# Two feed-forward products by one level of Strassen's algorithm

## The chip, the core and the metric

The kernel runs on one core of a Trainium2 chip. The metric is the device time of one execution in microseconds (us); of several runs the median is given. The core has five engines with queues of their own: TensorE (PE: matmuls, and weight loads that overlap them), VectorE (DVE), ScalarE (ACT), GpSimd (POOL) and SyncE (SP, which here issues DMAs). Matmuls write to PSUM, which has eight banks of 512 fp32 columns on 128 partitions; DVE and ACT read it, POOL does not here.

## The reference

The input x has 512 tokens of width 1024, in fp32. A first block (two attention branches, gated and merged) is followed by two layers, each of a feed-forward part, a mixer and a second feed-forward part, each of them with a residual and a layer norm. The change touches the four feed-forward parts:

```
def swiglu_half(x, w1, w3, w2):
    return 0.5 * ((jax.nn.silu(x @ w1) * (x @ w3)) @ w2)
...
x = layer_norm(ALPHA * x + swiglu_half(x, ffn2_w1[l], ffn2_w3[l], ffn2_w2[l]), ln3_g[l], ln3_b[l])
```

w1 and w3 are 1024 x 2816, w2 is 2816 x 1024. Everything is fp32.

## The kernel before, in words

**Products.** A full fp32 product is made of three faster ones. `split` (L212) cuts an operand into a high part, rounded to the type fp32r by ACT (L214), and the rest, a subtraction on DVE (L215). `mm3` (L248) then adds low x high, high x low and high x high in PSUM, through `mm` (L166), which all matmuls of the kernel share: in the profile they are L167 and are told apart by their tiles. The input of a layer stands transposed in `xTh` and `xTl` (features on partitions, 8 x 512 columns), made by `next_tile` (L767) with PE transposes (L307) from the residual `xr`.

**Weights.** A `Piece` (L217) loads a slab of a weight in two halves by SP's queue into `wst` and splits each half into `wh` and `wl`. In the feed-forward part w1 and w3 come from one pool (three `wst`, five `wh` and `wl` buffers, L775), w2 from another (`WP`, L238).

**Feed-forward.** The 2816 hidden features are cut into 11 blocks of 256. For a block, `hidden` computes (w1 block)^T x and (w3 block)^T x, 128 features by 512 tokens in a PSUM bank of pool `mm` at a time, 24 matmuls of 512 columns each. `act` (L787) takes Silu of the first on ACT (L788), multiplies by the second on DVE (L789) and splits the result into `hh` and `hl`. Block 0 is done apart, by halves of 256 tokens (`hidden_half`, L792), so that its first half can start before all tokens are there; after a mixer that first half lies in the mixer's tail. Then the blocks go in pairs (1,2), (3,4) to (9,10): after both, `hh` times w2 gives for each of four tiles of 128 tokens and two halves of 512 columns one bank of pool `mx`, which DVE adds to `xr` (L848). After the last pair `lnorm` (L735) does residual and norm of a tile, and `next_tile` transposes it for the next part. `banks(esf, mm=3, mx=5)` shares out the eight banks.

**Order.** The code is written in plain program order. A framework plans each engine's queue from it: an instruction goes in when its operands and its buffer (one of `bufs` under its tag) are ready by the planner's account, with earlier code first among those that are ready. It also sets the semaphores. Matmuls of a later product may thus stand between those of an earlier one. On the chip each queue is worked off in the planned order, and an instruction that has to wait holds up all that stands behind it.

Of the kernel before, what the change touches and what calls it, by code (L numbers as in the profile page):

```python
# [10 lines left out]
F32 = mybir.dt.float32  # L11
F32R = mybir.dt.float32r
# [121 lines left out]
def build(ctx, tc, A, out, stage="all"):  # L134
# [20 lines left out]
    def weights(es, nst, nw, side="left"):  # L155

        return pool(es, nm("w"), side, LINE), nst, nw

    def nm(s):
        uid[0] += 1  # L160
        return f"{s}{uid[0]}"

    def pool(es, name, side="left", line=SPAN):
        return Aligned(es.enter_context(tc.tile_pool(name=name, bufs=1, side=side, reuse_waits="tile")), line)

    def mm(o, a, b, start=True, stop=True):  # L166
        PE.matmul(o, a, b, start=start, stop=stop)  # L167

    B = {}

    def banks(es, **n):

        B.clear()
        for name, bufs in n.items():
            B[name] = es.enter_context(tc.tile_pool(name=nm("ps" + name), bufs=bufs, space=PSUM, reuse_waits="tile"))
# [4 lines left out]
    def mmbank():  # L180
        return bank("mm")

    def mxbank():
        return bank("mx")
# [27 lines left out]
    def split(hi, lo, src, eng=None):  # L212

        S.activation(hi, src, AF.Copy)  # L214
        V.tensor_sub(lo, src, hi.bitcast(F32))  # L215

    class Piece:  # L217


        def __init__(self, src, k0, nk, c0, ncol, w=None):  # L220
            wp, nst, nw = w or WP
            wp = wp.pool
            self.hk = nk // 2
            self.parts = []
            for h in range(2):
                r = (k0 + h * self.hk) * 128
                st = wp.tile([128, self.hk, ncol], F32, tag="wst", name=nm("wst"), bufs=nst)
                nc.sync.dma_start(st, src[r:r + self.hk * 128, c0:c0 + ncol].rearrange("(k p) c -> p k c", p=128))
                hi = wp.tile([128, self.hk, ncol], F32R, tag="wh", name=nm("wh"), bufs=nw)
                lo = wp.tile([128, self.hk, ncol], F32R, tag="wl", name=nm("wl"), bufs=nw)  # L230
                split(hi, lo, st)
                self.parts.append((hi, lo))
# [12 lines left out]
        for f in todo:  # L245
            f()

    def mm3(o, ah, al, bh, bl, start, stop):  # L248
        mm(o, al, bh, start, False)
        mm(o, ah, bl, False, False)  # L250
        mm(o, ah, bh, False, stop)

    def ws_block(src, c0, nm_, sink, nk=8, xh=None, xl=None):

# [38 lines left out]
    def nat(t):  # L293
        return slice(t * 128, (t + 1) * 128)
# [437 lines left out]
        return nxt  # L732


    def lnorm(t, po, scale, g, b, pl, done):  # L735

        xs = A["xr"][:, t, :]
        st = pl.tile([128, 4], F32, tag="lnst", name=nm("lnst"), bufs=2)
        s0, s1, nmu, rs = (st[:, i:i + 1] for i in range(4))
        hs = [slice(h * 512, (h + 1) * 512) for h in range(2)]  # L740
        for h in range(2):
            V.tensor_tensor_reduce(out=xs[:, hs[h]], in0=po(h), in1=xs[:, hs[h]], scale=scale, scalar=0.0 if h == 0 else s0,  # L742
                                   op0=ALU.add, op1=ALU.add, accum_out=s0 if h == 0 else s1)
        V.tensor_scalar(out=nmu, in0=s1, scalar1=-1.0 / D, scalar2=None, op0=ALU.mult)  # L744
        xn = pl.tile([128, D], F32, tag="lnx", name=nm("lnx"), bufs=1)
        sq = pl.tile([128, D], BF16, tag="lnq", name=nm("lnq"), bufs=1)
        S.activation(sq, xs, AF.Square, bias=nmu, accum_out=rs)  # L747
        powhalf(rs, rs, 1.0 / D, 1e-5)
        V.scalar_tensor_tensor(out=xn, in0=xs, scalar=nmu, in1=g, op0=ALU.add, op1=ALU.mult)
        for h in range(2):  # L750
            V.scalar_tensor_tensor(out=xs[:, hs[h]], in0=xn[:, hs[h]], scalar=rs, in1=b[:, hs[h]], op0=ALU.mult, op1=ALU.add)  # L751
            if done:
                done(t, h)
# [2 lines left out]
        hc = slice(h * 512, (h + 1) * 512)  # L756
        nc.sync.dma_start(out[0, nat(t), hc], A["xr"][:, t, hc])

    def ln_rows(pl, names, l):
        o = []  # L760
        for n in names:
            r = pl.tile([128, D], F32, name=nm("lnr"))
            nc.scalar.dma_start(r, rows(A[n][l]))
            o.append(r)
        return o
# [6 lines left out]
    def open_ffn(l, f, pre=None):  # L772

        es, w = pre[0:2] if pre else (ExitStack(), None)
        w = w or weights(es, 3, 5, "right")  # L775
        return es, w, [Piece(A[f"{f}_{n}_2"][l], 0, 8, 0, 256, wp) for n, wp in (("w1", w), ("w3", WP if pre else w))], []

    def hidden_tiles(pl, bufs):
        return tuple(pl.tile([128, 2, T], F32R, tag=n, name=nm(n), bufs=bufs) for n in ("hh", "hl"))

    def prod(o, pc, j, n0, n1):
        for k in range(8):
            wh, wl = pc.at(k)
            mm3(o, wh[:, j * 128:(j + 1) * 128], wl[:, j * 128:(j + 1) * 128], xTh[:, k, n0:n1],
                xTl[:, k, n0:n1], k == 0, k == 7)

    def act(sa, pa, pb, oh, ol):  # L787
        S.activation(sa, pa, AF.Silu)  # L788
        V.tensor_mul(sa, sa, pb)  # L789
        split(oh, ol, sa)  # L790

    def hidden_half(pl, pre, n0, bufs, sa=None):  # L792

        if not pre[3]:
            pre[3].extend(hidden_tiles(pl, bufs))
        hh, hl = pre[3]
        ab = [mmbank().rearrange("p (j n) -> p j n", j=2) for _ in range(2)]
        for i in range(2):
            for j in range(2):
                prod(ab[i][:, j, :], pre[2][i], j, n0, n0 + 256)  # L800
        sa = (pl.tile([128, T], F32, tag="sa", name=nm("sa"), bufs=2) if sa is None else sa).rearrange("p (j n) -> p j n", j=2)
        act(sa, ab[0], ab[1], hh[:, :, n0:n0 + 256], hl[:, :, n0:n0 + 256])

    def ffn(l, f, ln, pre, ahead=None, scale=None):

        w1, w3, w2 = (A[f"{f}_{w}_2"][l] for w in ("w1", "w3", "w2"))
        xr = A["xr"]
        es, wf = pre[0:2]
        nxt = None
        esf = ExitStack()  # L810
        banks(esf, mm=3, mx=5)
        fp = pool(esf, nm("ffn"), "right", LINE)
        g, b = ln_rows(fp, (ln + "_g_2", ln + "_b_2"), l)

        def hidden(c):

            if c == 0:
                for n0 in (256,) if pre[3] else (0, 256):
                    hidden_half(fp, pre, n0, 3)
                return pre[3]  # L820
            pcs = [Piece(w, 0, 8, c * 256, 256, wf) for w in (w1, w3)]
            hh, hl = hidden_tiles(fp, 3)
            for j in range(2):
                ab = [mmbank() for _ in range(2)]
                for i in range(2):
                    prod(ab[i], pcs[i], j, 0, T)
                act(fp.tile([128, T], F32, tag="sa", name=nm("sa"), bufs=2), ab[0], ab[1], hh[:, j, :], hl[:, j, :])
            return hh, hl

        for cs in ((0,), (1, 2), (3, 4), (5, 6), (7, 8), (9, 10)):  # L830
            hs = [hidden(c) for c in cs]
            p2 = [Piece(w2, 2 * c, 2, 0, 1024, wf if c == 10 else WP) for c in cs]
            if 10 in cs and ahead:
                nxt = ahead(pre)
            nk = 2 * len(cs)
            for t in range(NT):
                pos = []
                for h in range(2):
                    po = mxbank()
                    for k in range(nk):  # L840
                        hh, hl = hs[k // 2]
                        wh, wl = p2[k // 2].at(k % 2)
                        mm3(po, hh[:, k % 2, nat(t)], hl[:, k % 2, nat(t)], wh[:, h * 512:(h + 1) * 512],
                            wl[:, h * 512:(h + 1) * 512], k == 0, k == nk - 1)
                    pos.append(po)
                    if 10 not in cs:
                        xs = xr[:, t, h * 512:(h + 1) * 512]
                        V.tensor_add(xs, xs, po)  # L848
                if 10 in cs:
                    if t > 0 and ahead:  # L850
                        next_tile(t - 1, scale)
                    lnorm(t, lambda h: pos[h], 0.5, g, b, fp, None if ahead else put_out)
        if ahead:
            next_tile(3, scale)
        esf.close()
        if not nxt or nxt[0] is not es:
            es.close()
        return nxt
# [4 lines left out]
    def mixer(l, pre, ahead=None, scale=None):  # L863
# [655 lines left out]
                next_tile(t - 1, scale)  # L1519
            lnorm(t, lambda h: po[h], 1.0, g, b, P4, None if ahead else put_out)  # L1520
        if ahead:
            hidden_half(pool(nxt[0], nm("hid"), "right", LINE), nxt, 0, 1,
                        P4.tile([128, D], F32, tag="lnx", name=nm("sa"), bufs=1)[:, 0:T])
            B["mx"] = B["gd"]
            next_tile(2, scale)
            next_tile(3, scale)
# [51 lines left out]
```

## Time and profile before

| | us |
|---|---|
| median of three runs | 2771.26 (2770.39 to 2771.97) |
| the profiled execution | 2771.1 |
| span of its instructions | 2769.3 |
| PE busy | 2722.5 |
| DVE busy | 1399.8 |
| ACT busy | 999.7 |
| POOL busy | 185.8 |

The span runs from the first instruction's start to the last one's end. Matmuls overlap, so that a matmul's busy time is longer than the distance to the next one; distances between starts are read from the timeline. "L215" is line 215 of the kernel before, "mx<-wh,hl" an instruction that writes tile mx from tiles wh and hl, "128*128 128x512" a matmul with a 128x128 weight and 512 columns. The idle time before an instruction, and what ended it, stands behind a bar or in brackets.

### The profile page before, as it was taken

Reading aid. Unit: us, or ns where it says so; the run is one execution under the profiler, and the core shown is the slowest. Engines: PE = TensorE matmul, PEld = TensorE weight load, DVE = VectorE, ACT = ScalarE, POOL = GpSimd, SP = SyncE. Lnnn points to the kernel's source line nnn. Section 1 sums busy time; section 2 is a strip of 40 time slices with the busy share of each in tenths; the row PEclk is TensorE's granted clock in tenths of the full one; section 3 lists DMA queues with packets and bytes.
Section 4 is the critical chain, followed back from the end, with each engine's and each line's share of the span. In section 5 each row is a group of like instructions: output and inputs, shape, how many; then the busy total and the mean of one; then the engine's idle time right before and its main releaser. Section 6 shows DMA issues by size and latency. Waiting matters only on the chain. (4 is left out here: it accounts for less than half of the span.)

```text
span 2769.3 us, 36863 instructions
## 1 busy us (share of the span) xinstructions
PE 2722.5 (98%) x14736; PEld 2224.0 (80%) x14736; DVE 1399.8 (51%) x2698; ACT 999.7 (36%) x1607; POOL 185.8 (7%) x319
## 2 busy tenths in 40 slices
PE   8999999999999999999999999999999999999998
PEld 6779887888888887777888888888887777788887
DVE  6655555344433346865633435334354866643334
ACT  4444553333222234553422224222234553422222
POOL 1000013000000001110100000000000201100000
PEclk9999999999999999999999999999999999999999
DMA  5122222343333223224423333333323323433331
GB/s 165 47 77 70 69 77 88 104 156 101 104 102 91 76 87 91 64 72 138 128 92 95 102 101 99 91 92 97 102 66 89 94 59 129 132 97 92 92 91 46
DMA packets 195003, 260.64 MB, mean 94 GB/s; under 512 B 14376, under 2 KB 153264, under 8 KB 194768
## 3 DMA queue, kind: packets, MB, share of 16 engines
q1 hardware_dynamic: 169200, 221.55, 27.0%
q10 hardware_dynamic: 25632, 36.74, 4.1%
q8 instruction: 116, 1.90, 0.3%
q14 instruction: 55, 0.45, 0.0%
HBM read 246.09 MB, written 11.11 MB: 93 GB/s over the span
## 5 line engine op out<-in xcount | busy, mean ns | idle before, releaser
L215 DVE TENSOR_TENSOR wl<-wst,wh 128x1024 fp32r<-128x1024 f32 (+2 forms) x434 | 516.3, 1192 | 521.4 <-ACT wh L214 520.7
L167 PE MATMUL mm<-xTh,wl 128*128 128x512 f32 (+1 forms) x1984 | 749.6, 378 | 2.2 <-ACT xTh L214 2.1
L167 PE MATMUL mm<-xTl,wh 128*128 128x512 f32 (+1 forms) x1984 | 749.5, 378 | 0.6 <-DVE xTl L215 0.6
L167 PE MATMUL mm<-xTh,wh 128*128 128x512 f32 (+1 forms) x1984 | 746.4, 376 | 0.0
L214 ACT ACTIVATE wh<-wst 128x1024 fp32r<-128x1024 f32 (+2 forms) x434 | 438.9, 1019 | 778.4 <-PE mx L167 327.1
L167 PEld LDWEIGHTS mm<-xTh,wl 128*128 128x128 f32 x1984 | 373.7, 189 | 70.7 <-ACT xTh L214 2.6
L167 PEld LDWEIGHTS mm<-xTl,wh 128*128 128x128 f32 x1984 | 373.8, 188 | 70.3 <-issue 2.9
L167 PEld LDWEIGHTS mm<-xTh,wh 128*128 128x128 f32 x1984 | 373.8, 188 | 66.5
L167 PE MATMUL mx<-wh,hl 128*128 128x512 f32 x704 | 276.6, 393 | 0.0
L167 PE MATMUL mx<-wl,hh 128*128 128x512 f32 x704 | 274.1, 389 | 0.0
L167 PE MATMUL mx<-wh,hh 128*128 128x512 f32 x704 | 271.5, 390 | 0.0
L167 PE MATMUL mm<-wh,xTl 128*128 128x512 f32 (+2 forms) x640 | 254.0, 398 | 0.4 <-DVE xTl L215 0.4
L167 PE MATMUL mm<-wl,xTh 128*128 128x512 f32 (+2 forms) x640 | 248.8, 389 | 0.0
L167 PE MATMUL mm<-wh,xTh 128*128 128x512 f32 (+2 forms) x640 | 245.7, 384 | 0.0
L848 DVE TENSOR_TENSOR xr<-xr,mx 128x512 f32<-128x512 f32 x160 | 109.5, 686 | 206.8 <-PE mx L167 206.8
L789 DVE TENSOR_TENSOR sa<-sa,mm 128x512 f32<-128x512 f32 x88 | 60.5, 687 | 276.7 <-PE mm L167 276.7
L167 PEld LDWEIGHTS mm<-wl,xTh 128*128 128x128 f32 x640 | 144.7, 226 | 18.2 <-issue 5.8
L167 PEld LDWEIGHTS mm<-wh,xTl 128*128 128x128 f32 x640 | 144.2, 226 | 18.7 <-issue 5.2
L167 PEld LDWEIGHTS mx<-wh,hl 128*128 128x128 f32 x704 | 132.1, 188 | 32.3 <-DVE hl L215 5.7
L167 PEld LDWEIGHTS mm<-wh,xTh 128*128 128x128 f32 x640 | 144.7, 226 | 14.5 <-issue 1.8
L167 PEld LDWEIGHTS mx<-wh,hh 128*128 128x128 f32 x704 | 132.1, 188 | 27.8
L167 PEld LDWEIGHTS mx<-wl,hh 128*128 128x128 f32 x704 | 132.2, 188 | 26.5
(396 smaller groups left out, 2731.7 us busy)
## 6 DMA issues: line engine op xcount, KB each, us to landing
wst<-in_ffn_w_dram SPq DMA_DIRECT2D x264, 512.0 KB, 3.7
wst<-in_w_in_dram SPq DMA_DIRECT2D x106, 512.0 KB, 3.7
wst<-in_w_out_dram SPq DMA_DIRECT2D x24, 512.0 KB, 3.4
xd<-xr ACTq DMA_DIRECT2D x8, 512.0 KB, 2.6
wst<-in_w_in_dram SPq DMA_DIRECT2D x16, 256.0 KB, 2.8
lnr<-in_ln_g_dram ACTq DMA_DIRECT2D x6, 512.0 KB, 4.2
lnr<-in_ln_b_dram ACTq DMA_DIRECT2D x6, 512.0 KB, 6.0
ya<-xd ACTq DMA_DIRECT2D x10, 256.0 KB, 2.9
```

The source lines that it names most:

```text
L167: PE.matmul(o, a, b, start=start, stop=stop)
L214: S.activation(hi, src, AF.Copy)
L215: V.tensor_sub(lo, src, hi.bitcast(F32))
L789: V.tensor_mul(sa, sa, pb)
L848: V.tensor_add(xs, xs, po)
```

## The change

In blocks 1 to 10 the two products with w1 and w3 are done by one level of Strassen's algorithm (in Winograd's form). The weight block (1024 x 256) is cut into quarters of 512 x 128, the input (1024 features x 512 tokens) into quarters of 512 x 256. Instead of eight products of quarters there are seven, between sums of quarters; each product is four k-steps of `mm3` with 256 columns.

`Combos` takes the place of the two `Piece`s. It loads the same bytes, forms four sums of weight quarters on POOL and splits the quarter 11, two pairs of sums and the lower half. `strassen` does the seven products of one weight in two banks, two accumulators in each, and combines them: ACT copies the first product (`p1`), DVE forms `u2`, `u3` and three of the four result quarters; the fourth is read straight from PSUM by `first`. `sums` makes the four sums of input quarters once a feed-forward part, three subtractions and additions on POOL and the rest on DVE, and writes one of them over the quarter of `xTh` and `xTl` that nothing else reads after block 0. Its temporaries use the tags `tst` (also of `Combos`) and `sa` (also of the gated result).

The second product takes the first block's part for tiles 0 and 1 ahead of the rest (`early`). The banks become 4 and 4; `hh` and `hl` get two buffers instead of three, the `wh` and `wl` of w1 and w3 four instead of five; the rows of the norm are loaded with the last pair, into `tst`, and `lnorm` uses `sa` and `cb`. Block 0 is as it was.

```
...
-    def mm(o, a, b, start=True, stop=True):
-        PE.matmul(o, a, b, start=start, stop=stop)
+    def mm(o, a, b, start=True, stop=True, go_on=False):
+        PE.matmul(o, a, b, start=start, stop=stop, skip_group_check=go_on)
...
-    def mm3(o, ah, al, bh, bl, start, stop):
-        mm(o, al, bh, start, False)
-        mm(o, ah, bl, False, False)
-        mm(o, ah, bh, False, stop)
+    def mm3(o, ah, al, bh, bl, start, stop, go_on=False):
+        mm(o, al, bh, start, False, go_on)
+        mm(o, ah, bl, False, False, go_on)
+        mm(o, ah, bh, False, stop, go_on)
...
-    def lnorm(t, po, scale, g, b, pl, done):
+    def lnorm(t, po, scale, g, b, pl, done, tags=(("lnx", 1), ("lnq", 1))):
...
-        xn = pl.tile([128, D], F32, tag="lnx", name=nm("lnx"), bufs=1)
-        sq = pl.tile([128, D], BF16, tag="lnq", name=nm("lnq"), bufs=1)
+        (tx, bx), (tq, bq) = tags
+        xn = pl.tile([128, D], F32, tag=tx, name=nm("lnx"), bufs=bx)
+        sq = pl.tile([128, D], BF16, tag=tq, name=nm("lnq"), bufs=bq)
...
-            r = pl.tile([128, D], F32, name=nm("lnr"))
+            r = pl.tile([128, D], F32, name=nm("lnr"), **how)
...
-        w = w or weights(es, 3, 5, "right")
-        return es, w, [Piece(A[f"{f}_{n}_2"][l], 0, 8, 0, 256, wp) for n, wp in (("w1", w), ("w3", WP if pre else w))], []
+        w = w or weights(es, 3, 4, "right")
+        return es, w, [Piece(A[f"{f}_{n}_2"][l], 0, 8, 0, 256, wp) for n, wp in (("w1", w), ("w3", WP if pre else w))], [], pre[4] if pre else []
...
-            pre[3].extend(hidden_tiles(pl, bufs))
+            pre[3].extend(hidden_tiles(*((pre[4][0], 1) if pre[4] else (pl, bufs))))
...
+    class Combos:
+        def __init__(self, src, c0, w, pl):
+            wp, nst, nw = w[0].pool, w[1], w[2]
+            st = []
+            for h in range(2):
+                a = wp.tile([128, 4, 256], F32, tag="wst", name=nm("wst"), bufs=nst)
+                nc.sync.dma_start(a, src[h * 512:(h + 1) * 512, c0:c0 + 256].rearrange("(k p) c -> p k c", p=128))
+                st.append(a)
+            q11, q12, q21, q22 = (st[h][:, :, 128 * m:128 * m + 128] for h in range(2) for m in range(2))
+            ta, tb = (pl.tile([128, 2, 4, 128], F32, tag="tst", name=nm("tst"), bufs=2) for _ in range(2))
+            t3, t2, t1, t4 = ta[:, 0], ta[:, 1], tb[:, 0], tb[:, 1]
+            for o, x, y in ((t3, q22, q12), (t1, q11, q12), (t2, t1, q22), (t4, t2, q21)):
+                G.tensor_tensor(out=o, in0=x, in1=y, op=ALU.add)
+            def parts(shape, src, p, tags, bufs):
+                hi, lo = (p.tile(shape, F32R, tag=tag, name=nm(tag), bufs=bufs) for tag in tags)
+                split(hi, lo, src)
+                return hi, lo
+            one = parts([128, 4, 128], q11, pl, ("w1h", "w1l"), 2)
+            a = parts([128, 2, 4, 128], ta, wp, ("wh", "wl"), nw)
+            b = parts([128, 2, 4, 128], tb, wp, ("wh", "wl"), nw)
+            r = parts([128, 4, 256], st[1], wp, ("wh", "wl"), nw)
+            self.of = {"11": one, "21": [x[:, :, 0:128] for x in r], "22": [x[:, :, 128:256] for x in r],
+                       "t3": [x[:, 0] for x in a], "t2": [x[:, 1] for x in a],
+                       "t1": [x[:, 0] for x in b], "t4": [x[:, 1] for x in b]}
+    def strassen(cb, xs, pl, first, rest):
+        xa, ya = mmbank(), mmbank()
+        x0, x1, y0, y1 = xa[:, 0:256], xa[:, 256:512], ya[:, 0:256], ya[:, 256:512]
+        def q(o, w, x, start=False):
+            (wh, wl), (xh, xl) = cb.of[w], xs[x]
+            for k in range(4):
+                mm3(o, wh[:, k], wl[:, k], xh(k), xl(k), start and k == 0, k == 3, True)
+        def u(n, bufs):
+            return pl.tile([128, 256], F32, tag=n, name=nm(n), bufs=bufs)
+        p1, u2, u3 = u("p1", 2), u("u2", 2), u("u3", 1)
+        q(x0, "11", "11", True)
+        S.activation(p1, x0, AF.Copy)
+        q(y0, "t3", "s3", True)
+        q(x1, "t2", "s2")
+        V.tensor_tensor(out=u2, in0=x1, in1=p1, op=ALU.add)
+        q(y1, "t1", "s1")
+        V.tensor_tensor(out=u3, in0=y0, in1=u2, op=ALU.add)
+        V.tensor_tensor(out=rest[:, 512:768], in0=y1, in1=u3, op=ALU.subtract)
+        q(x0, "21", "12")
+        first(x0)
+        q(y0, "t4", "22")
+        q(y1, "22", "s4")
+        V.tensor_tensor(out=rest[:, 0:256], in0=y0, in1=u2, op=ALU.add)
+        V.tensor_tensor(out=rest[:, 256:512], in0=y1, in1=u2, op=ALU.subtract)
+    def sums(pl):
+        def quarter(i, j):
+            return [a[:, 4 * i:4 * i + 4, 256 * j:256 * j + 256] for a in (xTh, xTl)]
+        a11, a12, a21, a22 = quarter(0, 0), quarter(1, 0), quarter(0, 1), quarter(1, 1)
+        sh, sl = (pl.tile([128, 3, 4, 256], F32R, name=nm(n)) for n in ("sh", "sl"))
+        def f(a):
+            return a.bitcast(F32)
+        def tmp(tag):
+            return pl.tile([128, 4, 256], F32, tag=tag, name=nm("sf"), bufs=2)
+        d, e = tmp("tst"), tmp("tst")
+        G.tensor_tensor(out=d, in0=f(a11[0]), in1=f(a21[0]), op=ALU.subtract)
+        G.tensor_tensor(out=e, in0=f(a11[1]), in1=f(a21[1]), op=ALU.subtract)
+        G.tensor_tensor(out=d, in0=d, in1=e, op=ALU.add)
+        split(sh[:, 2], sl[:, 2], d)
+        d, e = tmp("sa"), tmp("sa")
+        V.tensor_tensor(out=d, in0=f(a21[0]), in1=f(a22[0]), op=ALU.subtract)
+        V.tensor_tensor(out=e, in0=f(a21[1]), in1=f(a22[1]), op=ALU.subtract)
+        V.tensor_tensor(out=d, in0=d, in1=e, op=ALU.add)
+        V.tensor_tensor(out=e, in0=d, in1=f(a11[0]), op=ALU.subtract)
+        V.tensor_tensor(out=e, in0=e, in1=f(a11[1]), op=ALU.subtract)
+        split(sh[:, 1], sl[:, 1], e)
+        split(sh[:, 0], sl[:, 0], d)
+        V.tensor_tensor(out=e, in0=e, in1=f(a12[0]), op=ALU.add)
+        V.tensor_tensor(out=e, in0=e, in1=f(a12[1]), op=ALU.add)
+        split(a21[0], a21[1], e)
...
-        banks(esf, mm=3, mx=5)
+        banks(esf, mm=4, mx=4)
         fp = pool(esf, nm("ffn"), "right", LINE)
-        g, b = ln_rows(fp, (ln + "_g_2", ln + "_b_2"), l)
+        ops = {}
         def hidden(c):
             if c == 0:
                 for n0 in (256,) if pre[3] else (0, 256):
-                    hidden_half(fp, pre, n0, 3)
+                    hidden_half(fp, pre, n0, 2)
+                ops.update(sums(fp))
                 return pre[3]
-            pcs = [Piece(w, 0, 8, c * 256, 256, wf) for w in (w1, w3)]
-            hh, hl = hidden_tiles(fp, 3)
-            for j in range(2):
-                ab = [mmbank() for _ in range(2)]
-                for i in range(2):
-                    prod(ab[i], pcs[i], j, 0, T)
-                act(fp.tile([128, T], F32, tag="sa", name=nm("sa"), bufs=2), ab[0], ab[1], hh[:, j, :], hl[:, j, :])
+            c1, c3 = (Combos(w, c * 256, wf, fp) for w in (w1, w3))
+            hh, hl = hidden_tiles(pre[4][0], 1) if pre[4] and c % 2 == 0 else hidden_tiles(fp, 1 if pre[4] else 2)
+            sa = fp.tile([128, D], F32, tag="sa", name=nm("sa"), bufs=2)
+            cb = fp.tile([128, 768], F32, tag="cb", name=nm("cb"), bufs=1)
+            strassen(c1, ops, fp, lambda x: S.activation(sa[:, 0:256], x, AF.Silu), sa[:, 256:1024])
+            S.activation(sa[:, 256:1024], sa[:, 256:1024], AF.Silu)
+            strassen(c3, ops, fp, lambda x: V.tensor_mul(sa[:, 0:256], sa[:, 0:256], x), cb)
+            V.tensor_mul(sa[:, 256:1024], sa[:, 256:1024], cb)
+            split(hh, hl, sa.rearrange("p (j n) -> p j n", j=2))
             return hh, hl
         for cs in ((0,), (1, 2), (3, 4), (5, 6), (7, 8), (9, 10)):
             hs = [hidden(c) for c in cs]
             p2 = [Piece(w2, 2 * c, 2, 0, 1024, wf if c == 10 else WP) for c in cs]
+            if 10 in cs:
+                g, b = ln_rows(fp, (ln + "_g_2", ln + "_b_2"), l, tag="tst", bufs=2)
             if 10 in cs and ahead:
                 nxt = ahead(pre)
             nk = 2 * len(cs)
+            def part(po, t, h, ks):
+                for k in ks:
+                    hh, hl = hs[k // 2]
+                    wh, wl = p2[k // 2].at(k % 2)
+                    mm3(po, hh[:, k % 2, nat(t)], hl[:, k % 2, nat(t)], wh[:, h * 512:(h + 1) * 512],
+                        wl[:, h * 512:(h + 1) * 512], k == 0, k == nk - 1)
+            early = {}
+            for t, h in ((t, h) for t in range(2) for h in range(2)):
+                early[t, h] = mxbank()
+                part(early[t, h], t, h, range(2))
             for t in range(NT):
                 pos = []
                 for h in range(2):
-                    po = mxbank()
-                    for k in range(nk):
-                        hh, hl = hs[k // 2]
-                        wh, wl = p2[k // 2].at(k % 2)
-                        mm3(po, hh[:, k % 2, nat(t)], hl[:, k % 2, nat(t)], wh[:, h * 512:(h + 1) * 512],
-                            wl[:, h * 512:(h + 1) * 512], k == 0, k == nk - 1)
+                    po = early.get((t, h)) or mxbank()
+                    part(po, t, h, range(2 if (t, h) in early else 0, nk))
...
-                    lnorm(t, lambda h: pos[h], 0.5, g, b, fp, None if ahead else put_out)
+                    lnorm(t, lambda h: pos[h], 0.5, g, b, fp, None if ahead else put_out, (("sa", 2), ("cb", 1)))
...
-            hidden_half(pool(nxt[0], nm("hid"), "right", LINE), nxt, 0, 1,
+            nxt[4].append(pool(nxt[0], nm("hid"), "right", LINE))
+            hidden_half(nxt[4][0], nxt, 0, 1,
                         P4.tile([128, D], F32, tag="lnx", name=nm("sa"), bufs=1)[:, 0:T])
...
```

## Rows read from the trace of the kernel before

**Rows 1.** The page: busy us (share) xinstructions; 40 slices, busy and granted clock in tenths.
```profile
PE 2722.5 (98%) x14736; PEld 2224.0 (80%) x14736; DVE 1399.8 (51%) x2698; ACT 999.7 (36%) x1607; POOL 185.8 (7%) x319
...
PE   8999999999999999999999999999999999999998
...
PEclk9999999999999999999999999999999999999999
```
**Rows 2.** Windows over two pairs of blocks: stretch, us, busy (count) by engine, clock, DMA.
```profile
1421.50:1486.90 65.40, 65.40 (x290) 53.97 (x288) 25.35 (x29) 16.98 (x20) 0.00 (x0) 1.00 0.32 97
...
1852.40:1917.80 65.40, 65.40 (x289) 53.96 (x288) 25.35 (x28) 16.98 (x20) 0.00 (x0) 1.00 0.33 97
```
**Rows 3.** Timeline of PE: start us, busy us, engine, line, operation, tiles, shape, count.
```profile
2396.97 0.28 PE L167 MATMUL mm<-xTh,wh 128*128 128x256 f32 x1
...
2407.41 0.29 PE L167 MATMUL mm<-xTh,wh 128*128 128x256 f32 x1
...
2423.35 0.40 PE L167 MATMUL mx<-wh,hl 128*128 128x512 f32 x1
...
2434.26 0.39 PE L167 MATMUL mm<-xTl,wh 128*128 128x512 f32 x1
```
**Rows 4.** Groups by form on DVE: xcount, busy us, mean ns, idle before <-releaser.
```profile
L215 DVE TENSOR_TENSOR wl<-wst,wh 128x1024 fp32r<-128x1024 f32 x394 | 488.2, 1241 | 440.2 <-ACT wh L214 439.7
L848 DVE TENSOR_TENSOR xr<-xr,mx 128x512 f32<-128x512 f32 x160 | 109.5, 686 | 206.8 <-PE mx L167 206.8
L215 DVE TENSOR_TENSOR hl<-sa,hh 128x512 fp32r<-128x512 f32 x88 | 60.6, 688 | 31.4 <-ACT hh L214 31.4
...
L215 DVE TENSOR_TENSOR xTl<-mm,xTh 128x256 fp32r<-128x256 f32 x16 | 6.7, 419 | 0.2
```
**Rows 5.** Groups by form on ACT.
```profile
L214 ACT ACTIVATE wh<-wst 128x1024 fp32r<-128x1024 f32 x394 | 413.4, 1057 | 734.7 <-PE mx L167 327.1 <-PE mm L167 253.6 <-DMA wst<-in_ffn_w_dram 89.3
...
L788 ACT ACTIVATE sa<-mm 128x512 f32<-128x512 f32 x88 | 52.3, 594 | 173.5 <-PE mm L167 171.8 <-DVE xr L751 1.7
...
L214 ACT ACTIVATE xTh<-mm 128x256 fp32r<-128x256 f32 x16 | 6.1, 383 | 24.8 <-DVE xTl L215 15.6 <-PE mm L1454 8.9
```
**Rows 6.** Groups by form on POOL.
```profile
L703 POOL TENSOR_TENSOR sgm<-sgm,sgm 128x512 f32<-128x512 f32 x8 | 11.2, 1419 | 106.8 <-DVE sgm L702 78.0 <-issue 28.7
...
L1046 POOL TENSOR_TENSOR msc<-msc,gng 128x1024 f32<-128x1024 f32 x2 | 4.8, 2378 | 64.2 <-DMA wst<-in_w_in_dram 32.3 <-ACT msc L1045 31.9
```
**Rows 7.** Timelines of POOL and of DVE where both work at once.
```profile
469.86 1.30 POOL L674 TENSOR_TENSOR y<-y,gateb 128x512 f32<-128x512 f32 x1
471.12 3.52 POOL L673 TENSOR_TENSOR y<-y,y 128x512 f32<-128x512 f32 x2
...
471.18 2.32 DVE L215 TENSOR_TENSOR wl<-wst,wh 128x1024 fp32r<-128x1024 f32 x1
...
590.79 3.53 POOL L703 TENSOR_TENSOR sgm<-sgm,sgm 128x512 f32<-128x512 f32 x2 [10.61 <-DVE sgm L702]
...
591.79 1.37 DVE L215 TENSOR_TENSOR wl<-wst,wh 128x1024 fp32r<-128x1024 f32 x1 [0.55 <-ACT wh L214]
593.09 1.77 DVE L215 TENSOR_TENSOR ml<-sgm,mh 128x512 fp32r<-128x512 f32 x1
```
**Rows 8.** Timeline: a product's last matmul and the reader of its bank.
```profile
1488.03 0.39 PE L167 MATMUL mx<-wh,hh 128*128 128x512 f32 x1
...
1488.46 0.69 DVE L848 TENSOR_TENSOR xr<-xr,mx 128x512 f32<-128x512 f32 x1 [0.90 <-PE mx L167]
```
**Rows 9.** Timeline of DVE at the start of a feed-forward layer.
```profile
2411.23 1.29 DVE L215 TENSOR_TENSOR xTl<-mx,xTh 128x512 fp32r<-128x512 f32 x2 [0.55 <-ACT xTh L214]
...
2424.34 0.68 DVE L789 TENSOR_TENSOR sa<-sa,mm 128x512 f32<-128x512 f32 x1
...
2426.67 0.69 DVE L215 TENSOR_TENSOR hl<-sa,hh 128x512 fp32r<-128x512 f32 x1
```
**Rows 10.** The page's DMA issues: tiles, queue, xcount, KB each, us to landing.
```profile
lnr<-in_ln_b_dram ACTq DMA_DIRECT2D x6, 512.0 KB, 6.0
```

More of the change, by code (lines that the diff above doesn't have):

```diff
@@ L757, in put_out, with ln_rows @@
         nc.sync.dma_start(out[0, nat(t), hc], A["xr"][:, t, hc])
-    def ln_rows(pl, names, l):
+    def ln_rows(pl, names, l, **how):
         o = []
         for n in names:
-            r = pl.tile([128, D], F32, name=nm("lnr"))
+            r = pl.tile([128, D], F32, name=nm("lnr"), **how)
             nc.scalar.dma_start(r, rows(A[n][l]))
@@ new lines, in sums, with of @@
+    def sums(pl):
[23 more added lines that the diff above has]
+        split(a21[0], a21[1], e)
+        def of(pair):
+            return [lambda k, a=a: a[:, k, :] for a in pair]
+        return {"11": of(a11), "12": of(a12), "22": of(a22), "s4": of(a21),
+                **{f"s{i + 1}": of((sh[:, i], sl[:, i])) for i in range(3)}}
```

## The prediction

> **What bounds the kernel now.** I read the page's busy shares first: TensorE (PE) is busy 98% of the span at full granted clock (1.0, the 2.4 GHz level), VectorE (DVE) 51%, ScalarE (ACT) 36%, GpSimd (POOL) 7% [rows 1]. A share is an average over stages, so I then read the windows of single stretches: one pair of hidden blocks in the feed-forward layer takes 65.40 us, and PE is busy for all of it, while DVE works 25.4 us, ACT 17.0, POOL nothing [rows 2]. The feed-forward layers are therefore bound by the number of matmuls times their spacing. Only fewer PE microseconds can shorten them, and everything that the change gives to DVE, ACT and POOL is free exactly as long as PE does not wait for it.
>
> **PE's part.** A busy time is no spacing (matmuls overlap), so I take start times. 512 columns: 48 matmuls from 2423.35 to 2434.26, 0.2273 us each. 256 columns with a fresh 128x128 weight each, the form that the change needs: 87 from 2396.97 to 2407.41, 0.120 us each [rows 3]. One weight of one block had 2 x 8 x 3 = 48 matmuls of 512 columns, 48 x 0.2273 = 10.91 us; now it has 7 products x 4 x 3 = 84 of 256, 84 x 0.120 = 10.08 us. Strassen's 12.5% shrinks to 7.6%, because the spacing holds about 13 ns beside the columns and is paid 84 times instead of 48. The gain is 0.83 us a weight; with 2 weights, 10 blocks and 4 feed-forward layers, 80 x 0.83 = 66 us. It cannot be larger, since PE has no idle time there to win back. The second product keeps its matmuls; taking part of it early changes their order alone.
>
> The Trainium skill ("TensorE: Matmul & The Clock Gate", Back-to-back issue gap) gives N/2.4 + 2.5 ns, so 215.8 and 109.2 ns, and by it the gain would be 80 x (10.36 - 9.17) = 95 us. The starts in the trace are 227 and 120 ns apart, so the measurement decides, and I give that figure no chance.
>
> **What it adds to DVE, ACT and POOL.** Durations: on DVE 1.24 us for 1024 columns from SBUF, 0.69 for 512, 0.42 for 256 [rows 4]; on ACT 1.06 for 1024, 0.59 for 512, 0.38 for 256 [rows 5]; on POOL an addition of 512 takes 1.30 us with nothing beside it (the rows' means of 1.42 and 2.38, the latter for 1024, hold waits) [rows 6, 7]. A block in steady state:
> - POOL: 2 weights x 4 additions of 512 = 8 x 1.30 = 10.4 us, before 0.
> - DVE: splits of the weights 2 x (0.69 + 3 x 1.24) = 8.8; of the third weight 2.5; readers of the products, 11 of 256 columns, 4.6; product of 768 about 0.96 (between the rows); split of the hidden tile 1.24; four additions to the residual 2.8. Sum 20.9 us, before 25.4 / 2 = 12.7.
> - ACT: about 2 x (0.6 + 3 x 1.06 + 0.38) + 2.1 + 0.4 + 0.8 + 1.1 = 12.7 us, before 8.5.
>
> PE's time for a block becomes 2 x 10.08 + 10.91 = 31.07 us. None of the three engines fills that: 67%, 41%, 33%. But two of them exclude each other. At 590.79 two POOL additions take 3.53 us instead of 2.60, while the DVE splits beside them take 1.37 and 1.77 instead of 1.24 and 0.69; at 471.18 a DVE split of 1.24 takes 2.32, next to two POOL additions of together 3.52 [rows 7]. Whichever starts second waits for the first to end. DVE's two-input work on SBUF (13.5 us a block) and POOL's (10.4) are thus one queue of 23.9 us in 31.07. Readers of PSUM are outside it, yet stand behind it, as DVE takes its instructions in order.
>
> The Trainium skill says the same ("SBUF — State Buffer", Who interferes with whom): a DVE instruction with two SBUF inputs and a GpSimd instruction that reads SBUF block each other for a whole instruction. That rule speaks against this change, and the third rival below is what it would do; the rows bear it out.
>
> **Waits inside a weight's seven products.** They use two banks in turn. Two hand-overs are tight. The fifth product overwrites what u2 reads: 12 matmuls (1.44 us) of cover. The sixth overwrites the bank that u3 and the subtraction behind it read: again 1.44 us of cover. A reader starts 0.04 us after the last matmul's end [rows 8], which is 0.28 us after that matmul's start, so 0.20 us of cover are gone; taking 0.05 us back to PE, u2 (0.42) leaves 0.77 us, and the two readers (0.34 + 0.42) leave 0.43 us for whatever stands in front of them on DVE. ACT's copy of the first product (0.38) has 0.8 us, on a less busy engine: nothing. In front stands a weight split for about 0.6 of the time, with 0 to 1.6 us left of it (1.24, plus part of a POOL wait). Expected excess: 0.6 x 0.52 x 0.42 = 0.13 us and 0.6 x 0.73 x 0.58 = 0.25 us, 0.38 us a weight if PE has nothing else. It has: the next weight's first products use the other two banks and can be ordered ahead. So the bounds are 0 and one lengthened split at the tighter place each time (2.5 - 0.43 = 2.1 us, 166 us in all); I take half of 0.38, 80 x 0.19 = 15 us, near the lower bound, because the orders of before keep PE without any idle time with splits in flight [rows 2].
>
> **Start of a layer.** The four sums of input quarters (ten additions) come once a layer, between the last transpose and the first block's products. In the second layer's second feed-forward the input is complete at 2411.23 + 1.29 = 2412.5, and the sums take 11 DVE instructions of 1.24 (13.6 us) and three POOL additions of 2.4 (7.1 us). Two of their buffers are those of the first block's gated result, whose last reader ended at 2426.67 + 0.69 = 2427.4 [rows 9]; so the longer chain starts there. Four additions, ACT's 1.06 and a split: second sum at 2434.7; fourth at 2440.7. PE needs them at 2434.26 + 2 x 1.44 = 2437.1 and at 2434.26 + 6 x 1.44 = 2442.9. Between them stand the first block's eight additions to the residual (5.5 us, not to be put off with four banks), one or two weight splits (1.9) and up to four POOL additions (5.2): fourth sum at 2448 to 2453, 5 to 10 us late, less 2.9 us of the second weight's first two products. I take 5 us, 4 x 5 = 20 us in all; bounds 0 (all of it hidden by reordering) and 40.
>
> **Edits that I cost at nothing.** DMA moves the same bytes with the same instructions. One weight buffer fewer (5 to 4): the tightest slot, the third copy's, comes free after the sixth product of the weight before, 7.2 us before its own first use, and its split needs 2.3 us (ACT, then DVE); without that cover it would be 2.3 us a weight. The longer tail of a block (two readers, product of 768, two halves of the split: some 4.5 us) lies under the 24 early matmuls, 5.45 us; without them it would be 4 us a pair. Norm rows are loaded late, by ACT's queue: their landing takes 6.0 us [rows 10], the second product before their use 8 us; a landing that is not covered costs up to 6 us a layer, and an ACT copy queued behind the issue waits with it. One bank fewer for the second product: 0.69 us of addition under 1.36 us of matmuls; at a layer's end it may cost 1 or 2 us, which I leave to the range.
>
> **Sum.** The profiled run took 2771.1 us (span 2769.3 plus 1.8 around it), within 0.2 us of the median of 2771.26. 2771.1 - 66 + 15 + 20 = 2740 us.
>
> **Rivals.**
> 1. All covered: the ordering hides both kinds of wait but some 5 us. 2771.1 - 66 + 5 = 2710 us. For it: no PE idle time in any steady pair before. Against it: DVE goes from 39% to 67% there, with POOL in its way. 0.16.
> 2. Forecast: 2740, own range 2716 to 2766. 0.55.
> 3. Slower: DVE's and POOL's exclusive turns put a lengthened split in front of the product readers. Place: the sixth product. It decides from (66 - 20) / 80 = 0.57 us a weight; with every second weight paying 2.1 us, 80 x 1.05 = 84 us, and 2771.1 - 66 + 84 + 20 = 2809 us. For it: [rows 7]; at the worst POOL's whole 10.4 us adds to DVE's 20.9, which gives 31.3 us a block, more than PE's 31.07. Against it: the readers themselves touch SBUF with one input, and additions come in bursts. 0.17.
> 4. The sums stand bare: 20 us a layer instead of 5, because the planner puts weight work ahead of them. 2771.1 - 66 + 15 + 80 = 2800 us. Against it: 23 us lie between complete input and first need. 0.07.
> 5. The gains and waits cancel, 2766 to 2777: 0.05.
>
> **Numbers.** The likeliest is 2740 us. Below 2709 lies half of the first rival, above 2792 most of 3 and part of 4: about 0.08 and 0.12 are left out. A difference of 0.2% (5.5 us) is what can be told from none: faster 0.73, same 0.06, slower 0.21.
>
> **What would show it.** PE matmuls rise by 80 x 36 = 2880 to 17616, at 0.120 us where they have 256 columns. A steady pair takes 62.1 us plus its waits; DVE some 42 us in it, POOL 21. PE's idle time, named by a DVE reader of "mm" banks, is the 15 us; by the sums at four layer starts, the 20 us. The prediction is wrong if 256-column matmuls come further apart than 0.120 us, if PE waits more than 0.57 us a weight, or if a layer's start loses over 10 us.

## The result, and the profile after

The changed kernel takes 2857.55 us (median of four, 2851.72 to 2865.14), the kernel before 2770.88: a ratio of 1.0314, 95% interval 1.0302 to 1.0326. It is slower by 87 us where 31 us of gain were forecast, and the time lies outside the range. The page of the changed kernel, busy times by engine and the granted clock in 40 slices [rows 1 are those of before]:

```profile
PE 2706.9 (95%) x17616; PEld 2334.5 (82%) x17616; DVE 1821.9 (64%) x3262; ACT 1162.3 (41%) x1823; POOL 717.5 (25%) x651
...
PEclk9999999999999999999899999999999999999999
```

There are 2880 matmuls more, as worked out, and PE is nevertheless busy for less time: the products did become cheaper. PE waits instead, and the mean granted clock of the run is 0.986 (0.998 before). Its waits, longest first in total (engine, what it was about to write, what ended the wait: us in total, times, longest):

```profile
PE mx L167 <- DVE hl L215: 40.3, 21, 7.9
PE mm L167 <- DVE sa L858: 27.6, 31, 1.3
PE mm L167 <- DVE u L855: 13.6, 20, 1.2
PE mm L167 <- ACT p L852: 12.2, 5, 3.4
```

None of these four lines stands among the waits of the kernel before. L858 and L855 are the readers inside `strassen` (the subtraction behind u3, and u2), L852 is the copy of the first product; hl is the last step of a block's gated result. No wait for a copy of a weight is among PE's waits: the copies come in time, the readers come late.

A pair of blocks, the windows that answer to [rows 2]:

```profile
1467.60:1534.00 66.40, 62.69 (x428) 57.84 (x428) 42.59 (x55) 23.49 (x28) 24.80 (x16) 1.00 0.32 96
1854.20:1921.40 67.20, 62.86 (x428) 57.81 (x427) 43.32 (x54) 23.48 (x28) 25.58 (x16) 1.00 0.31 95
```

PE needs 62.1 us for such a pair and takes 66 to 67, at full clock, with DVE busy for 42.6 to 43.3 (42 were forecast) and POOL for 24.8 to 25.6 (21 were forecast). What happens in one of the waits shows on the timelines of POOL, DVE and PE:

```profile
1472.39 1.29 POOL L823 TENSOR_TENSOR tst<-wst 128x512 f32<-128x512 f32 x1 [22.78 <-DVE wl L215]
1473.76 4.38 POOL L823 TENSOR_TENSOR tst<-tst,wst 128x512 f32<-128x512 f32 x2
...
1471.09 1.23 DVE L215 TENSOR_TENSOR wl<-tst,wh 128x1024 fp32r<-128x1024 f32 x1 [0.75 <-ACT wh L214]
1472.23 0.42 DVE L857 TENSOR_TENSOR u<-mm,u 128x256 f32<-128x256 f32 x1
1472.56 2.20 DVE L215 TENSOR_TENSOR wl<-wst,wh 128x1024 fp32r<-128x1024 f32 x1
1474.68 0.41 DVE L858 TENSOR_TENSOR sa<-mm,u 128x256 f32<-128x256 f32 x1
...
1473.91 0.28 PE L167 MATMUL mm<-xTh,w1h 128*128 128x256 f32 x1
1474.03 0.28 PE L167 MATMUL mm<-sh,wl 128*128 128x256 f32 x1
1475.15 0.38 PE L167 MATMUL mm<-xTh,wl 128*128 128x256 f32 x1 [0.84 <-DVE sa L858]
```

A POOL addition starts at 1472.39, a weight split on DVE 0.17 us later. The split takes 2.20 us instead of 1.24, as it waits for POOL's addition to end; L858 stands behind it, and PE's sixth product behind L858. Two splits are in L858's way, one in front of u3 (L857) and the lengthened one between u3 and L858. And PE has already done other work in the meantime: the next weight's first product (`w1h`) stands between the fifth and the sixth product. Both hold for all 31 waits for L858: two splits stand in front, 3.2 to 3.5 us together, with one of them lengthened, and 12 matmuls of the next weight's first product stand ahead of the sixth.

POOL also delays a split at the end of a pair:

```profile
1514.72 1.29 POOL L823 TENSOR_TENSOR tst<-wst,wst 128x512 f32<-128x512 f32 x1 [2.78 <-DMA wst<-in_ffn_w_dram]
...
1515.02 2.07 DVE L215 TENSOR_TENSOR hl<-sa,hh 128x1024 fp32r<-128x1024 f32 x1 [1.13 <-ACT hh L214]
...
1517.14 0.50 PE L167 MATMUL mx<-wh,hl 128*128 128x512 f32 x1 [1.24 <-DVE hl L215]
```

And over the whole run (groups by form; the first line answers to the first of [rows 4], the POOL lines to [rows 6]) the splits of loaded weights take 1.39 us on average instead of 1.24, the split of the gated result 1.74, and POOL's additions 1.38 to 1.69 instead of 1.30:

```profile
L215 DVE TENSOR_TENSOR wl<-wst,wh 128x1024 fp32r<-128x1024 f32 x314 | 435.6, 1391 | 338.6 <-ACT wh L214 338.0
...
L215 DVE TENSOR_TENSOR hl<-sa,hh 128x1024 fp32r<-128x1024 f32 x40 | 69.7, 1742 | 24.7 <-ACT hh L214 24.6
...
L823 POOL TENSOR_TENSOR tst<-tst,wst 128x512 f32<-128x512 f32 x160 | 270.3, 1689 | 12.5
...
L823 POOL TENSOR_TENSOR tst<-wst 128x512 f32<-128x512 f32 x80 | 110.2, 1377 | 470.8 <-DVE wl L215 460.2
```

The start of the last feed-forward layer, timelines of DVE (answering to [rows 9]), ACT and PE, then the window of the wait:

```profile
2480.33 3.81 DVE L215 TENSOR_TENSOR w1l<-wst,w1h 128x512 fp32r<-128x512 f32 x2 [0.66 <-ACT w1h L214]
...
2498.47 0.68 DVE L790 TENSOR_TENSOR sa<-sa,mm 128x512 f32<-128x512 f32 x1
...
2503.37 0.68 DVE L215 TENSOR_TENSOR hl<-sa,hh 128x512 fp32r<-128x512 f32 x1
```
```profile
2501.05 1.06 ACT L214 ACTIVATE wh<-tst 128x1024 fp32r<-128x1024 f32 x1 [5.98 <-POOL tst L823]
2502.01 0.61 ACT L214 ACTIVATE hh<-sa 128x512 fp32r<-128x512 f32 x1
```
```profile
2504.10 0.80 PE L167 MATMUL mx<-wh,hl 128*128 128x512 f32 x1 [6.35 <-DVE hl L215]
2504.69 0.63 PE L167 MATMUL mx<-wl,hh 128*128 128x512 f32 x1
2505.12 0.63 PE L167 MATMUL mx<-wh,hh 128*128 128x512 f32 x1
```
```profile
2499.00:2510.00 11.00, 5.90 (x14) 4.66 (x15) 8.61 (x11) 2.64 (x3) 5.22 (x4) 0.53 0.30 95
```

The product (L790) of block 0's second half stood behind three weight splits and one of the sums on DVE until 2498.47. Then ACT waited 5.98 us for a POOL sum before a copy of a weight, and the copy of the gated result stood behind that. PE was idle for 6.35 us. In the window the granted clock is 0.53 on average, and from 2504.1 to 2510.0 it is 0.50, the 1.2 GHz level: 13 matmuls start 0.43 us apart there instead of 0.227.

The first pair of each layer has a wait that the later pairs don't have. ACT stands for a POOL sum, the copy of the first product (L852) stands behind that, and PE waits for the copy. This makes 11.9 of the 12.2 us of L852 above, 2.8 to 3.4 us in each layer:

```profile
1420.66 1.06 ACT L214 ACTIVATE wh<-tst 128x1024 fp32r<-128x1024 f32 x1 [3.27 <-POOL tst L823]
1421.62 0.36 ACT L852 ACTIVATE p<-mm 128x256 f32<-128x256 f32 x1
...
1422.04 0.58 PE L167 MATMUL mm<-sh,wl 128*128 128x256 f32 x1 [2.80 <-ACT p L852]
```

Where the 87 us went (us, sums over the four layers). A pair ends with the start of its last addition to `xr`, a norm with the start of the last L742 of its last tile. The columns e1, e2 and e10 are runs below (e2 its single run, e10 the profile of the timed runs):

| stretch | before | after | e1 | e2 | e10 |
|---|---|---|---|---|---|
| up to block 0's last addition (the attention block at the start included) | 780.6 | 828.3 | 803.8 | 818.4 | 783.2 |
| blocks 1 and 2, four pairs | 262.0 | 279.9 | 246.9 | 242.0 | 284.1 |
| blocks 3 to 8, twelve pairs | 785.1 | 804.0 | 768.4 | 767.2 | 742.6 |
| last pair and norm | 276.0 | 270.5 | 265.9 | 265.7 | 266.2 |
| two mixers | 658.4 | 666.5 | 661.6 | 661.1 | 656.8 |

Work moves between the rows. In e10 work of blocks 3 and 4 is ordered ahead into the first pair, so the second and third row are to be added there. In the changed kernel, e1 and e2 the first row holds 126 to 136 matmuls of 256 columns more than before, which are block 1's, done ahead: at 0.12 us each some 15 us of the row are not lost.

### The profile page after: what moved, and what is told of

Same layout as the page of the kernel before. It is cut to its first block, busy times and chain, and to the rows that moved or that the text cites. A ratio compares the mean times of both kernels' runs of the same rounds, so it can differ in the third digit from the quotient of the medians.

```text
span 2856.3 us, 43990 instructions
## 1 busy us (share of the span) xinstructions
PE 2706.9 (95%) x17616; PEld 2334.5 (82%) x17616; DVE 1821.9 (64%) x3262; ACT 1162.3 (41%) x1823; POOL 717.5 (25%) x651
## 5 line engine op out<-in xcount | busy, mean ns | idle before, releaser
L215 DVE TENSOR_TENSOR wl<-wst,wh 128x1024 fp32r<-128x1024 f32 (+1 forms) x354 | 463.7, 1314 | 416.8 <-ACT wh L214 416.3
L214 ACT ACTIVATE wh<-wst 128x1024 fp32r<-128x1024 f32 (+1 forms) x354 | 354.3, 1010 | 729.8 <-PE mx L167 271.5
L167 PE MATMUL mm<-xTh,wl 128*128 128x256 f32 (+1 forms) x1664 | 534.6, 321 | 43.4 <-DVE sa L858 27.6
L167 PE MATMUL mm<-xTl,wh 128*128 128x256 f32 (+1 forms) x1664 | 523.7, 315 | 0.7 <-DVE xTl L215 0.7
L167 PE MATMUL mm<-xTh,wh 128*128 128x256 f32 (+1 forms) x1664 | 520.8, 313 | 0.0
L167 PE MATMUL mm<-sh,wl 128*128 128x256 f32 x960 | 274.6, 287 | 12.2 <-ACT p L852 12.2
L167 PE MATMUL mm<-sl,wh 128*128 128x256 f32 x960 | 274.4, 286 | 0.2 <-DVE sl L215 0.2
L167 PE MATMUL mm<-sh,wh 128*128 128x256 f32 x960 | 273.8, 286 | 0.0
L823 POOL TENSOR_TENSOR tst<-tst,wst 128x512 f32<-128x512 f32 x160 | 270.3, 1689 | 12.5
L215 DVE TENSOR_TENSOR wl<-tst,wh 128x1024 fp32r<-128x1024 f32 x160 | 215.0, 1344 | 56.4 <-ACT wh L214 56.3
```

What stands on the lines that cost most here:

```text
L167: PE.matmul(o, a, b, start=start, stop=stop, skip_group_check=go_on)
L823: G.tensor_tensor(out=o, in0=x, in1=y, op=ALU.add)
```

## The experiments

Theory A: POOL's additions and DVE's two-input instructions on SBUF exclude each other; a lengthened instruction stands in front of a reader for which PE waits. Theory B: DVE has too much to do, or its order is bad, whatever POOL does. The single runs stand beside 2769.83 us of the kernel before on the same chip, e11 beside 2770.59.

**e1, no additions on POOL.**

```
-            for o, x, y in ((t3, q22, q12), (t1, q11, q12), (t2, t1, q22), (t4, t2, q21)):
-                G.tensor_tensor(out=o, in0=x, in1=y, op=ALU.add)
+            ta, tb = (x.rearrange("p k (m c) -> p m k c", m=2) for x in st)
```

> Left out: the four additions of weight quarters on POOL; the splits of the pairs take the loaded quarters instead (other values, the same number of splits). Theory A (exclusive turns: a POOL addition lengthens a DVE split from 1.24 to about 2.1 us, and that split stands in front of a product's reader): a steady pair falls from 66.3-67.4 us to 62.1-63.5 and the whole to about 2775 us. Theory B (DVE's own load and planned order are enough, POOL or not): a pair stays at 66 us or more and the whole above 2840.

Measured 2755.96 us, 102 less than the changed kernel; a pair takes 64.0 us on average. That is A and not B, although a pair stays 0.5 us above A's range and the whole comes out 19 us below its figure. One pair's window, without POOL:

```profile
1792.50:1856.70 64.20, 62.93 (x434) 58.39 (x433) 38.73 (x56) 24.72 (x30) 0.00 (x0) 1.00 0.33 99
```

**e2, the additions on DVE.** One letter: `G.tensor_tensor` becomes `V.tensor_tensor` in that loop.

> The same four additions, on DVE instead of POOL: DVE gets 8 x 0.69 = 5.5 us a block more, POOL nothing. Theory A: no split is lengthened any more, a pair takes 62.5 to 64.5 us, the whole 2790 to 2815. Theory B: DVE goes from 42.7 to 53 us in a pair and PE waits more: a pair takes 68 us or more, the whole above 2890.

Measured 2763.61 us, 26 us below A's range; a pair takes 63.9, inside it. DVE has more to do than in the changed kernel and PE waits less, which contradicts B:

```profile
1863.30:1926.80 63.50, 62.77 (x434) 58.36 (x432) 48.44 (x71) 24.73 (x30) 0.00 (x0) 1.00 0.33 100
```

By the trace, the order on DVE is not the reason either. In e2 some DVE instruction stands between u3 and the subtraction behind it (L858) at 76 of the 80 weights, in the changed kernel at 31. Yet PE's waits for L858 fall from 27.6 us to 7.9; no split between the two takes longer than 1.22 us in e2.

Timed later:

> The same kernel as e2 (the weights' four additions on DVE, otherwise the changed kernel), timed: 2758 to 2768 us, a ratio of 0.996 to 0.999. If the one look was luck of the clock, the ratio's interval holds 1.

2766.79 us (ten runs, 2758.85 to 2773.75), ratio 0.9989, interval 0.9976 to 1.0003. It holds 1: against the kernel before e2 is no gain that can be told, against the changed kernel about 90 us.

**e7, POOL's additions with nobody to read them.** e1's splits, and beside them the old additions into `tst`.

> As e1 (the splits take the loaded quarters), but POOL makes its four additions a weight again and nothing reads them: POOL's traffic without anyone waiting for its results. If it is the exclusive turns with DVE that cost: a steady pair goes from 63.5-64.5 us in e1 back to 66-67.5, splits of 1.24 us are lengthened to about 2 again, the whole 2830-2860 us. If it was the lateness of POOL's sums (the chain of four additions in front of the splits): a pair stays at 63.5-64.5, the whole at 2755-2775.

Measured 2892.2 us; a pair takes 68.7. Both lie above the first forecast's ranges and far from the second's. Nothing reads POOL's results here, so their lateness is not the cause in the steady pairs. Buffers still wait for POOL: at the end of each layer ACT's loads of the norm rows, which share the tag `tst`, stand until the additions are done, and PE loses 13 us in all behind ACT's copy of a first product. The additions also hold the loaded weights a little longer, and part of the rise may come from that. Groups by form of DVE, e7 and then e1:

```profile
L215 DVE TENSOR_TENSOR wl<-wst,wh 128x1024 fp32r<-128x1024 f32 x474 | 636.7, 1346 | 386.6 <-ACT wh L214 386.0
L215 DVE TENSOR_TENSOR w1l<-wst,w1h 128x512 fp32r<-128x512 f32 x80 | 83.4, 1045 | 20.7 <-ACT w1h L214 20.7
```
```profile
L215 DVE TENSOR_TENSOR wl<-wst,wh 128x1024 fp32r<-128x1024 f32 x474 | 587.0, 1241 | 388.0 <-ACT wh L214 387.1
L215 DVE TENSOR_TENSOR w1l<-wst,w1h 128x512 fp32r<-128x512 f32 x80 | 64.4, 808 | 33.8 <-ACT w1h L214 33.8
```

**e11, the same traffic in the kernel before.** In `hidden` four POOL additions a weight into one unread tile.

```
+            for pc in pcs:
+                q11, q12, q21, q22 = ...
+                for x, y in ((q22, q12), (q11, q12), (q11, q22), (q22, q21)):
+                    G.tensor_tensor(out=fp.tile([128, 4, 128], F32, tag="un", ...), in0=x, in1=y, op=ALU.add)
```

> The kernel before, with POOL making four additions of weight quarters (512 columns each) a weight, which nothing reads. If POOL's turns cost only where a reader has no cover: splits are lengthened here too, but a pair stays at 65.4 to 66.0 us and the whole at 2770-2785. If POOL's traffic in itself slows PE's supply: a pair takes 67 us or more, the whole above 2800.

Measured 2802.38 us, 32 more; a pair takes 66.4 instead of 65.4. A pair lies between the two forecasts, the whole in the second's range: even with DVE busy for 42% of a pair the turns cost 1.0 us a pair, at one place. The split of the gated result takes 1.22 us instead of 0.69 [rows 4], and in the window of one pair this is PE's only wait:

```profile
1824.20:1890.70 66.50, 65.56 (x289) 53.98 (x289) 28.09 (x29) 16.98 (x20) 24.65 (x16) 1.00 0.32 95
```
```profile
L215 DVE TENSOR_TENSOR hl<-sa,hh 128x512 fp32r<-128x512 f32 x88 | 107.5, 1222 | 31.4 <-ACT hh L214 31.4
```
```profile
PE mx L167 <- DVE hl L215: 0.9, 1, 0.9
```

The pairs make 17 of the 32 us. Another 14 lie at the layer starts: after each mixer the norm's last two instructions on DVE (L752) take 3.4 us beside POOL's additions instead of 1.4, PE waits 4.4 us for the split of its input, and the granted clock of the start is 0.92 instead of 1.00. From the waits of the whole run:

```profile
PE mx L308 <- DVE xTl L215: 8.8, 2, 4.4
```

**e3, no sums of the input.** `sums` returns quarters as they are.

> Left out: the sums of input quarters at the start of a feed-forward layer (quarters as they are stand in for them). If these sums make the late layer starts (47 us over the four, first product's hidden tile 5 to 8 us late and the clock at half after it): the starts come back to within 3 us each of the kernel before, the whole to 2805-2820 us. If it is the first Strassen block's own weight work that stands in front: starts stay 8 us or more late each, the whole above 2835. Steady pairs stay at 66.3-67.4 either way.

Measured 2824.87 us, between the two ranges. The first row of the table falls from 828.3 to 796.5, still 4 us a layer above before: two thirds of that row's rise go with the sums (some 14 of these 32 us are block 1's matmuls that are no longer done ahead). Most of the rest is at the two starts after a mixer, where the trace shows the same as in e11: L752 takes 3.4 us beside POOL's additions for the first Strassen block, PE waits 3.4 and 4.4 us for the split of its input, and the granted clock is 0.92. The twelve pairs stay at 67.3 us.

**e6, the products of w1 and w3 in turns.** `strassen` becomes a generator that yields after each product, and the two advance by turns.

> The products of w1 and w3 take turns (11 of w1, 11 of w3, and so on), so that each reader has two products (2.9 us) of cover instead of one (1.44). If the loss in steady pairs is late readers at the hand-overs: PE's waits for the readers fall to nearly nothing and a pair takes 62.5 to 64.5 us, the whole about 2815. If it is the copies of the weights that come late (four buffers now have to hold both weights' copies): a pair takes 66 us or more, with PE waiting for splits.

Measured 2923.78 us; a pair takes 72.2. The second forecast: PE waits for splits of the weights, and for the gated result. That the four buffers make them late was argued; no run changed their number. (Lines are one further down in this kernel.)

```profile
PE mx L168 <- DVE hl L216: 69.2, 20, 7.9
PE mm L168 <- DVE wl L216: 55.2, 33, 3.0
```

The readers' waits are gone from the longest lines, as twice the cover should make them, but the price is larger. It does not settle what the cover alone would bring.

**e8, e9, e10: towards a better version.** e8 is e2 with the input sums on DVE too. e9 and e10 do blocks 1 and 2, or block 1 alone, the old way and put the sums behind them (e10's edit; e9 has 2 in place of 1):

```
+            if not (c > 1):
+                pcs = [Piece(w, 0, 8, c * 256, 256, wf) for w in (w1, w3)]
...
+                if c == 1:
+                    ops.update(sums(fp))
+                return hh, hl
```

> As e2, and the three POOL additions of the input sums go to DVE too, so that POOL does nothing in the layer. If POOL's turns still delay the layer starts in e2 (48 us from the norm's end to the first block's last addition, 36.6 before): starts shorten by 2 to 5 us each, the whole 2745-2758. If DVE's own 13.6 us of sums are what is late: starts stay at 46-50 us, the whole 2760-2775.

> As e8, but blocks 1 and 2 are done the old way and the input sums follow them: 8 of 11 blocks by Strassen. If the layer start is late because sums and first weight work stand before the first block's gated result: starts return to 36-38 us, the first pair takes 65.4-66.5, the others 63-64, the whole 2740-2752. If the sums only move their lateness: the second pair takes 68 us or more, the whole above 2760.

> As e9 with block 1 alone done the old way: 9 of 11 blocks by Strassen. Same theory: starts 36-39 us, first pair 64-66, the whole 2736-2750, a few us under e9; if the sums are late for block 2, the first pair takes 68 us or more and the whole is above e9's.

Measured 2752.04, 2746.03 and 2734.72 us: e8 and e9 in the range of the first forecast, e10 1 us below its. e10's first pair takes 70.7 us, which the second forecast had, but for another reason: work done ahead for the next pair, which takes 57.6.

The table's first row is 801.5, 784.6 and (timed) 783.2. This is not the gain that it seems. e8's first row holds 161 matmuls of 256 columns more than before, some 19 of its 21 us, and PE's waits in it are 24.2 us, as before (22.9; 45.4 in the changed kernel), although the sums still stand in front, all on DVE. So it was POOL's part in this work that made PE wait, not DVE's. Without the mixers, whose code is the same, the rows add up to 2077.6 us in e8, 2084.9 in e9, and 2074.0 and 2076.1 in the two profiles of e10. The mixers take 665.4 in e8, 652.4 in e9, and 651.7 and 656.8 in e10, so that most of what e9 and e10 seem to gain on e8 lies there. e8 was run only once, so what moving the sums behind the first blocks brings is not shown. Timed:

> The same kernel as e10, timed against the kernel before: all weight and input sums on DVE, block 1 the old way. If the one look was right: 2733 to 2738 us, a ratio of 0.986 to 0.989 with an interval that leaves out 1.

2742.27 us (four runs, 2735.27 to 2743.18) beside 2770.59, ratio 0.9896, interval 0.9878 to 0.9914: 28 us faster than the kernel before, 115 than the changed one, though 4 us above the forecast. A pair late in a layer:

```profile
1920.10:1983.40 63.30, 62.79 (x434) 58.41 (x434) 48.46 (x71) 24.71 (x30) 0.00 (x0) 1.00 0.33 101
```

## Why the prediction was wrong

- **PE's part** was right: 256-column matmuls start 0.120 us apart, 2880 more of them, and e10's pair at 63.3 us beside 65.4 shows that the gain is there. The Trainium skill's formula ("TensorE: Matmul & The Clock Gate", Back-to-back issue gap), which I took for the spacing, would give 0.109 us; the page gives it for an isolated matmul, and the trace of this stream shows 0.120.
- **Waits inside the seven products** is the step that failed. I had the mechanism, the place (the sixth product, behind u3 and its subtraction) and the price of one case, and gave it 0.19 us a weight, 15 us in all. In the twelve middle pairs the loss is (804.0 - 785.1 + 12 x 3.3) / 48 = 1.2 us a weight. PE's waits on record there are some 45 us: 23.1 for the subtraction (L858), 8.2 for u2 (L855) and 13.8 for the gated result, which is the next point. The two readers alone make 0.65 us a weight. My sum let one split stand in front of a reader, with at most 1.6 us left, and took POOL's turns as a small addition to some splits. The trace has two splits there, one of them at about 2.1 us. I had halved 0.38 us because PE would fill the gap with the next weight's first product. It did so before every wait for L858, and that was not enough. Without POOL (e1) the waits in the twelve pairs are 12.2 us, 0.25 a weight; a pair's loss falls from (67.0 - 62.1) / 4 = 1.2 us a weight to (64.0 - 62.1) / 4 = 0.5. So POOL's turns cost 0.7 us a weight. The third rival, 2809 us at a chance of 0.17, named this mechanism and needed 0.57 us a weight to decide.
- **The longer tail of a block**, costed at nothing under 5.45 us of early matmuls, was not covered: PE waits for the gated result in each of the twelve pairs, 13.8 us in all. Its last split, 1.24 us in my sum, took 1.74 on average. In e1 the cover is enough (0.2 us).
- **ACT's copy of the first product**, costed at nothing, made PE wait for 12.2 us, nearly all in the first pairs, because the copy stands behind a wait for a POOL sum. The first pairs add 17.9 us over the layers.
- **Start of a layer**: 5 us each were forecast, the first row rose by 47.7 / 4 = 12. Some 15 of the 47.7 us are block 1's matmuls done ahead, and the loss is about 8 us a layer. I had the fourth sum decide. PE's waits there are for the first block's own gated result instead (7.9, 5.9 and 6.4 us at three of the starts), which stood behind sums, splits and POOL on DVE and on ACT; e8, with none of the sums on POOL, has no such wait at these starts. About 2.6 us of the last start (13 matmuls at 0.43 instead of 0.227) are the clock after the wait.
- **The mixers**, which I left out, took 8 us more. The second one's granted clock was 0.96 in the changed kernel and 1.00 before, the first one's 0.99 and 0.98; their code is the same but for the last lines. Why the clock fell there I can't say. Two executions of one kernel (e10) have 651.7 and 656.8 us in the mixers, so 8 us need not come from the change.
- The Trainium skill's rule on the shared SBUF access ("SBUF — State Buffer", Who interferes with whom), which I weighed, is borne out by the trace: a split beside a POOL addition takes 2.20 us instead of 1.24. By it the third rival should have had more weight.

## What to carry to other kernels

Work moved to GpSimd is not free beside VectorE instructions with two SBUF inputs: add the two as one queue, and then look at what stands behind the longest instruction of that queue, not at its load. Here the same additions cost some 90 us less on VectorE, although its load rose. When you estimate how long a reader is held up, count all instructions that the planned order may put in front of it, and between two readers of one bank, not only one. And when a stage seems to start late, count first whether it does more work there.

## What the runs showed of the hardware

- Two POOL additions beside DVE splits take 4.38 us instead of 2.60, and the split beside the POOL addition before them 2.20 instead of 1.24: these times fit with the one that starts second waiting until the other has ended.
- Unread POOL additions cost 32 us in a kernel whose DVE is busy for 42% of a pair (e11): 17 us in the pairs, by one wait of 0.9 us in most of them, and 14 at the layer starts.
- After an idle PE of 6.35 us the granted clock was 0.50 (1.2 GHz) for the next 5.9 us, and matmuls of 512 columns started 0.43 us apart.
